# One layer of a hybrid encoder on one core: two products of the gates in another order, the scale of the scores moved into the keys, deeper loads of the last weights, a held split, and another order of the first instructions

## The chip, the core and the metric

The kernel runs on one core of a Trainium2 chip. The core has a matrix engine (TensorE, PE in the profile), a vector engine (DVE), an engine for activations and copies (ACT), a general engine (POOL, GpSimd) and an engine that issues most of the transfers (SP). The metric is device time in microseconds. The kernel before takes 869.28 us, the median of three runs (869.12 to 870.82).

## The reference: what is computed

The input is 512 rows of 1024 float32 values, one layer deep. Cut to what the change touches:

```python
n = rms_norm(h, mix_norm_g)
proj = n @ w_in                                    # S5 input, gMLP halves, two gates
gate_a, gate_b = sigmoid(proj[.., GA:GB]), sigmoid(proj[.., GB:])
merged = gate_a * (ya @ w_proj_a) + gate_b * (yb @ w_proj_b)
h = h + merged @ w_out
# memory cross-attention, 4 heads of 256, 256 memory tokens
s = einsum('blhd,bmhd->bhlm', q, k) * 256 ** -0.5
p = softmax(s)
h = h + einsum('bhlm,bmhd->blhd', p, v) @ w_xo
h = h + (silu(hn @ w_gate) * (hn @ w_up)) @ w_down # d_ff = 2816
return rms_norm(h, final_norm_g)
```

All of it is in float32.

## The kernel before, in words

**Matrix products.** Each float32 operand is split into two parts that TensorE multiplies in one pass: `hi` is a rounded copy (ACT, a CAST at L85) and `lo` the rest (DVE, a subtraction at L86). A product is three passes, hi*hi, hi*lo and lo*hi (`mm3`, L396). Weights come by DMA as blocks of 512 KB into `wraw` tiles, of which there are three (tag `raw`), and are split into `whi` and `wlo`.

**Strassen products.** The larger products are computed as seven products of half the size (Winograd's form), numbered 1 to 7. `product` (L1241) runs one of them; the banks in which sums build up are named `gx`, `gv`, `gq` for the gates, `qx`, `qv`, `qq` for the queries, `px`, `pv`, `pq` for the feed-forward part and `dx`, `dv`, `dq` for the down projection.

**What sets the order.** `plan` is a list of weight blocks in the order of their use. Each entry has loads, with how many entries ahead of its use each is issued (`LOADS` is 3), and a function that makes the split tiles, two entries ahead (`SPLITS`). `next_w` takes the next entry and starts what is due. The framework then orders the instructions of each engine with a simulated timeline; `in_order` keeps some in the order of the code, and `tc.issue_after(x)` holds some behind an instruction x. SP issues its DMAs strictly in that order: one that waits for a buffer holds up those behind it.

**The places in question.**
- Start (L590 to L640): ten matmuls on ones (`idle`), then two products of ones with the row of g (`pg`, which spreads g over the partitions), the first 128 rows scaled by DVE with `r` and `pg`, and in two halves: `whi` of the first weight block, a copy of `pg` into `g_mix`, the transposes of the rows (`ptr`, L563) with their split into `xn`, and `wlo`.
- Gates (L1323 on): `gate_step(q, i)` runs product q for gate i, in the order of the table `ORDER`. Step 7 copies `gx` on ACT and subtracts it from `gq` on DVE (`u`, L1254). Steps 1, 2, 4, 6 and 7 write `gx` or `gv`, steps 5 and 3 write `gq`.
- Attention (`k_evac`, `scores`): key tiles are split from the bank into `kt_hi` and `kt_lo`; for each head and each half of the rows, the scores `psc` are reduced to a maximum `mx`, `nm` is -scale times it, ACT forms exp(scale*psc + nm) with the sum `sm`, DVE the reciprocal `rs` and the scaled `prob`, and TensorE transposes `prob` (`ppt`, L1545).
- Down projection (`plan_down`): 42 entries, seven products of six blocks each; products 1, 2 and 3 read w_down itself, 5, 6, 7 and 4 read sums of its blocks that DMAs have built up in memory before (`dsum`). The pool `stp` holds the buffers of the feed-forward units before it (tags `b21`, `t`, `b22`, two each).
- End (`onto_h`, `make_tokens`): `onto_h(dx, 2, 0, ...)` adds the two banks of `dx` to h; `row_by_row(4, 0)` behind it asks for the tokens of product 4, which are split from `a_low` into `s`.

## Time and profile before

| | before |
|---|---|
| median of three runs | 869.28 us (869.12 to 870.82) |
| profiled execution, whole | 870.48 us |
| its span, first to last instruction | 868.7 us |
| busy: PE, DVE, ACT, POOL | 855.1, 648.3, 474.8, 106.0 us |
| TensorE matmuls | 5894 |
| mean granted TensorE clock | 0.996 |
| moved by DMA | 155.40 MB, mean 179 GB/s |

The busy time of an engine is the time in which at least one of its instructions ran. A wait is put down to the instruction that released it. In a row of the timeline the first two numbers are the start and the time taken, then come engine, line, operation, output and inputs, and in brackets the idle time ahead of it and what ended it. In the table by stretch, a row has the stretch, its length, the busy time and count of each engine, the granted clock, the share of the DMA engines that was busy, and GB/s.

### The profile page before, as it was taken

How to read it: one execution, taken by the hardware profiler on the slowest of the kernel's cores; microseconds unless marked ns; L12 is line 12 of the kernel's file. 1: busy time of each engine (PE TensorE's matmuls, PEld its weight loads, DVE VectorE, ACT ScalarE, POOL GpSimd, SP SyncE). 2: the span in 40 equal slices, each digit the busy share in tenths (PEclk: the TensorE clock that was granted, in tenths of full speed). 3: DMA queues.
4: the chain of work that ended last, by engine and by line, in shares of the span. 5: the costliest groups of instructions: out<-in, count | busy, mean ns of one | idle time of the engine just before them, and what ended most of it. 6: DMA issues, size and time to landing. Idle time of an engine off the chain costs nothing.

```text
span 868.7 us, 14845 instructions
## 1 busy us (share of the span) xinstructions
PE 855.1 (98%) x5894; PEld 760.1 (88%) x5894; DVE 648.3 (75%) x897; ACT 474.8 (55%) x704; POOL 106.0 (12%) x157
## 2 busy tenths in 40 slices
PE   8999999999999999999999999999999999999996
PEld 6788888888789988899899888999999999987875
DVE  5699589968748668679658646767877778898875
ACT  5544875276437534467457444655545454655664
POOL 1001155100601000110010001001111111000000
PEclk9999999999999999999999999999999999999999
DMA  7549279745639586944687143557798786476572
GB/s 247 163 115 265 66 216 242 160 128 169 158 92 252 138 230 206 274 124 160 217 257 214 53 151 103 146 146 178 166 240 230 183 222 143 134 213 216 201 246 94
DMA packets 110119, 155.40 MB, mean 179 GB/s; under 512 B 8969, under 2 KB 77089, under 8 KB 109986
## 3 DMA queue, kind: packets, MB, share of 16 engines
q1 hardware_dynamic: 91746, 128.27, 44.9%
q0 software_dynamic: 18016, 25.66, 18.5%
q8 instruction: 46, 0.75, 0.3%
q10 hardware_dynamic: 288, 0.52, 0.2%
q14 instruction: 23, 0.19, 0.1%
HBM read 148.70 MB, written 37.20 MB: 214 GB/s over the span
## 4 chain that ended last, share of the span: by engine, by line
PE 91%; DMA 3%; ACT 2%; DVE 2%; issue 1%; SPq 0%; POOL 0%; POOLq 0%; ACTq 0%; DVEq 0%
PE pf L396 25%; PE pt L396 18%; PE px L1241 13%; PE dx L396 7%; PE pq L1241 6%; PE pv L1241 3%; PE gx L1241 3%; PE qx L1241 3%; PE dq L396 2%; PE gq L1241 1%; PE psc L396 1%; PE po L396 1%; PE qq L1241 1%; PE py L1034 1%; PE ptr L563 1%
## 5 line engine op out<-in xcount | busy, mean ns | idle before, releaser
L85 ACT CAST whi<-wraw 128x1024 fp32r<-128x1024 f32 (+1 forms) x133 | 136.9, 1029 | 143.1 <-PE pf L396 42.1
L86 DVE TENSOR_TENSOR wlo<-wraw,whi 128x1024 fp32r<-128x1024 f32 (+1 forms) x133 | 158.5, 1192 | 71.9 <-ACT whi L85 70.9
L396 PE MATMUL pf<-xn,whi 128*128 128x512 f32 x320 | 99.8, 392 | 0.0
L1241 PE MATMUL px<-fn,whi 128*128 128x256 f32 x480 | 83.2, 276 | 0.0
L1241 PEld LDWEIGHTS px<-fn,whi 128*128 128x128 f32 x480 | 72.5, 188 | 0.2
L396 PEld LDWEIGHTS pf<-xn,whi 128*128 128x128 f32 x320 | 59.6, 188 | 12.5 <-issue 0.5
L85 ACT CAST whi<-b 128x1024 fp32r<-128x1024 f32 x40 | 42.2, 1054 | 51.4 <-PE px L1241 26.5
L86 DVE TENSOR_TENSOR wlo<-b,whi 128x1024 fp32r<-128x1024 f32 x40 | 48.9, 1222 | 28.5 <-ACT whi L85 28.5
L1241 PE MATMUL px<-fn,wlo 128*128 128x256 f32 x240 | 66.4, 277 | 0.0
L396 PE MATMUL pf<-xn,wlo 128*128 128x512 f32 x160 | 62.9, 393 | 0.0
L1241 PE MATMUL pq<-s,whi 128*128 128x256 f32 x320 | 55.0, 276 | 0.0
L396 PE MATMUL dx<-whi,s 128*128 128x512 f32 x170 | 53.3, 391 | 0.4 <-DVE h L1876 0.4
L86 DVE TENSOR_TENSOR wlo<-t,whi 128x1024 fp32r<-128x1024 f32 x30 | 36.7, 1224 | 19.4 <-ACT whi L85 19.4
L85 ACT CAST whi<-t 128x1024 fp32r<-128x1024 f32 x30 | 31.6, 1054 | 35.3 <-PE pv L1241 12.6
L1241 PEld LDWEIGHTS pq<-s,whi 128*128 128x128 f32 x320 | 48.2, 188 | 0.0
L1241 PEld LDWEIGHTS px<-fn,wlo 128*128 128x128 f32 x240 | 45.1, 188 | 0.0
L1241 PE MATMUL pq<-s,wlo 128*128 128x256 f32 x160 | 44.2, 276 | 0.0
L396 PE MATMUL pt<-whi,xn 128*128 128x512 f32 x128 | 42.8, 407 | 0.3 <-ACT xn L85 0.2
L396 PEld LDWEIGHTS dx<-whi,s 128*128 128x128 f32 x170 | 31.8, 188 | 7.6 <-issue 0.8
L312 POOL DMA_DIRECT2D dsum<-in_w_down_dram x12 | 13.3, 1108 | 189.8 <-DMA dsum<-in_w_down_dram 189.8
L396 PEld LDWEIGHTS pf<-xn,wlo 128*128 128x128 f32 x160 | 30.1, 188 | 6.3 <-issue 0.2
L396 PE MATMUL dx<-wlo,s 128*128 128x512 f32 x85 | 32.9, 389 | 0.0
(480 smaller groups left out, 2329.5 us busy)
## 6 DMA issues: line engine op xcount, KB each, us to landing
wraw<-in_w_in_dram SPq DMA_DIRECT2D x35, 512.0 KB, 5.8
dsum<-in_w_down_dram SPq DMA_DIRECT2D x20, 512.0 KB, 5.9
wraw<-dsum SPq DMA_DIRECT2D x20, 512.0 KB, 3.7
b<-in_w_gate_dram SPq DMA_DIRECT2D x15, 512.0 KB, 4.3
b<-in_w_up_dram SPq DMA_DIRECT2D x15, 512.0 KB, 5.2
wraw<-in_w_down_dram SPq DMA_DIRECT2D x15, 512.0 KB, 4.8
dsum<-in_w_down_dram POOLq DMA_DIRECT2D x10, 512.0 KB, 7.5
dsum<-dsum POOLq DMA_DIRECT2D x10, 512.0 KB, 6.4
```

The lines of the kernel that those rows point to most:

```text
L85: hi = nc.scalar.copy(dst_hi, src)
L86: lo = nc.vector.tensor_tensor(dst_lo, src, dst_hi.bitcast(F32), ALU.subtract)
L312: plan[j + step][1].append((0, lambda d=dst, x=more: nc.gpsimd.dma_start(d, x, accum_op=ALU.add)))
L396: last_mm[0] = nc.tensor.matmul(ps, a[x], b[y], start=start and i == 0, stop=stop and i == 2, skip_group_check=free)
L563: tr = nc.tensor.transpose(ps[:, j, :], src[:, k * P:(k + 1) * P], ident)
L1034: in_order(nc.tensor.matmul(ps[64 * j:64 * j + 64, :], a, b, start=g % 4 == k == 0, stop=k == 2, tile_position=(0, 64 * j), skip_group_che ...
L1241: nc.tensor.matmul(ps[:, j, :], a[x], b[y], start=start and j == k == i == 0, stop=k == 3 and i == 2, skip_group_check=True)
```

## The change

Six edits:

1. `ORDER`: the steps (3, 0) and (4, 0) change places.
2. The key tiles are scaled by -1/16 as they are split, and the scores then need a minimum and no multiplication.
3. `plan_down`: from the third entry on a load takes one of nine buffers in turn (three `raw`, two each of `b21`, `t`, `b22`) and is issued six entries ahead.
4. `held_back`: the token splits that `make_tokens` writes for product 4 after `onto_h(dx, 2, 0, ...)` are held behind the first addition of the latter.
5. The first weight block is loaded by two DMAs of 256 KB (`parts=2`).
6. Three idle matmuls ahead of the products of g and six behind, rather than ten ahead; the first half's `whi` and `wlo` are issued first, then both copies into `g_mix`, then the first half's transposes, the second half's weights and transposes.

```diff
@@ -130,12 +130,13 @@
         pad = pool.tile([P, 48], F32, name="pad", bufs=1)
         nc.gpsimd.memset(pad, 0.0)
 
-    def plan_block(w, kb, k, c0, n, more=None, place=None):
+    def plan_block(w, kb, k, c0, n, more=None, place=None, parts=1):
         got = {}
 
         def load():
             got["raw"] = wp.tile([P, k, n], F32, tag="raw", name="wraw", bufs=3)
-            nc.sync.dma_start(got["raw"], block(w, kb, k, c0, n))
+            for i in range(0, k, k // parts):
+                nc.sync.dma_start(got["raw"][:, i:i + k // parts], block(w, kb + i, k // parts, c0, n))
 
         def make():
             if more is not None:
@@ -150,7 +151,7 @@
 
     def plan_tok(w, c0, nk, kpt=2):
         for kb in range(0, nk, kpt):
-            plan_block(w, kb, kpt, c0, 512)
+            plan_block(w, kb, kpt, c0, 512, parts=1 if plan else 2)
 
 
 
@@ -222,7 +223,7 @@
             plan.append(((w_q, 512 * n, q), [(LOADS, load)], lambda got=got: halves(got.pop("raw"))))
 
     GATES = [(w_in, OFF_GB), (w_in, OFF_GB + 512)]
-    ORDER = ((1, 0), (1, 1), (2, 0), (2, 1), (5, 0), (6, 0), (5, 1), (7, 0), (6, 1), (3, 0), (7, 1), (4, 0), (4, 1), (3, 1))
+    ORDER = ((1, 0), (1, 1), (2, 0), (2, 1), (5, 0), (6, 0), (5, 1), (7, 0), (6, 1), (4, 0), (7, 1), (3, 0), (4, 1), (3, 1))
     gate_place = [None]
 
     def plan_gates():
@@ -312,20 +313,23 @@
             plan[j + step][1].append((0, lambda d=dst, x=more: nc.gpsimd.dma_start(d, x, accum_op=ALU.add)))
 
     def plan_down(w, make_tokens, entries):
+        turns = ("raw", "b21", "raw", "t", "b22", "raw", "b21", "t", "b22")
         for q in DOWN:
             for c in range(CHUNKS):
                 got = {}
 
-                def load(q=q, c=c, got=got):
+                def load(q=q, c=c, got=got, n=len(entries)):
                     src = down_block(*DSRC[q], c) if q in DSRC else down_sum(q, c)
-                    got["raw"] = wp.tile([P, 2, 512], F32, tag="raw", name="wraw", bufs=3)[:, :src.shape[1]]
+                    tag = turns[n % len(turns)] if n > 1 else "raw"
+                    got["raw"] = (wp if tag == "raw" else stp[0]).tile(
+                        [P, 2, 512], F32, tag=tag, name="wraw", bufs=3 if tag == "raw" else 2)[:, :src.shape[1]]
                     nc.sync.dma_start(got["raw"], src)
 
                 def make(q=q, c=c, got=got):
                     make_tokens(q, c)
                     return halves(got.pop("raw"))
 
-                entries.append(((w, q, c), [(LOADS, load)], make))
+                entries.append(((w, q, c), [(LOADS if len(entries) < 2 else 6, load)], make))
 
     plan_tok(w_in, OFF_V, KD)
     for c0 in range(0, SW, 256):
@@ -597,7 +601,7 @@
         for i in range(n):
             in_order(nc.tensor.matmul(idle, ones, ones, start=True, stop=True))
 
-    idles(10)
+    idles(3)
     warm = np_.tile([P, 1], F32, tag="ms", name="warm", bufs=2)
     nc.scalar.activation(warm, mhalf, AF.Square)
 
@@ -619,18 +623,25 @@
         pg = [aux("pg") for i in range(2)]
         for i in range(2):
             in_order(nc.tensor.matmul(pg[i], ones[0:1, :], g_row[:, HALF[i]], start=True, stop=True))
+        idles(6)
         r = rms_factor(row_sums(xt[:, 0, :]))
         raw = plan[0][3].pop("raw")
         hi = wp.tile([P, 2, 512], F32R, tag="hi", name="whi", bufs=3)
         lo = wp.tile([P, 2, 512], F32R, tag="lo", name="wlo", bufs=3)
         pinned[0] = True
+
+        def weights(q):
+            in_order(nc.scalar.copy(hi[:, q, :], raw[:, q, :]))
+            in_order(nc.vector.tensor_tensor(lo[:, q, :], raw[:, q, :], hi[:, q, :].bitcast(F32), ALU.subtract))
+
         for i in range(2):
             in_order(nc.vector.scalar_tensor_tensor(xt[:, 0, HALF[i]], xt[:, 0, HALF[i]], r, pg[i], ALU.mult, ALU.mult))
-        for q in range(2):
-            in_order(nc.scalar.copy(hi[:, q, :], raw[:, q, :]))
-            in_order(nc.scalar.copy(g_mix[:, HALF[q]], pg[q]))
-            to_feat(xt[:, 0, :], xn_hi, xn_lo, slice(0, P), part=(q,))
-            in_order(nc.vector.tensor_tensor(lo[:, q, :], raw[:, q, :], hi[:, q, :].bitcast(F32), ALU.subtract))
+        weights(0)
+        for i in range(2):
+            in_order(nc.scalar.copy(g_mix[:, HALF[i]], pg[i]))
+        to_feat(xt[:, 0, :], xn_hi, xn_lo, slice(0, P), part=(0,))
+        weights(1)
+        to_feat(xt[:, 0, :], xn_hi, xn_lo, slice(0, P), part=(1,))
         tiles.append((hi, lo))
 
     first_rows()
@@ -1460,8 +1471,11 @@
     kt_lo = ap_.tile([P, KD, M], F32R, name="kt_lo")
     vts = []
 
+    scale = XD ** -0.5
+
     def k_evac(m, j, ps):
-        split(kt_hi[:, m, :], kt_lo[:, m, :], ps)
+        nc.scalar.activation(kt_hi[:, m, :], ps, AF.Copy, scale=-scale)
+        nc.vector.scalar_tensor_tensor(kt_lo[:, m, :], ps, -scale, kt_hi[:, m, :].bitcast(F32), ALU.mult, ALU.subtract)
 
     def v_evac(half):
         def f(t, ps):
@@ -1512,7 +1526,6 @@
 
     def scores(hd, behind=None):
         q_hi, q_lo = qs.pop(hd)
-        scale = XD ** -0.5
         prob = ap_.tile([P, NT, M], F32, tag="prob", name="prob", bufs=1) if hd % 2 == 0 else \
             np_.tile([P, NT, M], F32, tag="gain", name="prob", bufs=2)
         for i in range(2):
@@ -1524,12 +1537,11 @@
                     with nullcontext() if behind is None else tc.issue_after(behind):
                         mm3(ps[:, tt, :], (q_hi[:, k, tsl], q_lo[:, k, tsl]),
                             (kt_hi[:, 2 * hd + k, :], kt_lo[:, 2 * hd + k, :]), k == 0, k == 1)
-            mx, nm, sm, rs = (ap_.tile([P, 2], F32, tag=k, name=k, bufs=4) for k in ("mx", "nm", "sm", "rs"))
-            nc.vector.tensor_reduce(mx, ps, AX.X, ALU.max)
-            nc.vector.tensor_scalar(nm, mx, -scale, None, ALU.mult)
+            nm, sm, rs = (ap_.tile([P, 2], F32, tag=k, name=k, bufs=4) for k in ("nm", "sm", "rs"))
+            nc.vector.tensor_reduce(nm, ps, AX.X, ALU.min)
             for tt in range(2):
                 nc.scalar.activation(prob[:, 2 * i + tt, :], ps[:, tt, :], AF.Exp, bias=nm[:, tt:tt + 1],
-                                     scale=scale, accum_out=sm[:, tt:tt + 1])
+                                     scale=-1.0, accum_out=sm[:, tt:tt + 1])
             nc.vector.reciprocal(rs, sm)
             for tt in range(2):
                 nc.vector.tensor_scalar(prob[:, 2 * i + tt, :], prob[:, 2 * i + tt, :], rs[:, tt:tt + 1], None, ALU.mult)
@@ -1738,7 +1750,7 @@
 
 
 
-    made, last_job = {}, []
+    made, last_job, held_back = {}, [], [None]
 
     def token_pieces(f, ts, c):
         if c < 2:
@@ -1753,7 +1765,8 @@
         hi, lo = made[q, c] = sums_place((1, 2, 4)[len(made) % 3], 4, 256)
         f, ts = {1: (0, T0), 5: (0, T1), 6: (0, T1), 2: (1, T0), 7: (0, T0), 3: (1, T0), 4: (1, T1)}[q]
         for src, ks in token_pieces(f, ts, c):
-            split(hi[:, ks], lo[:, ks], src)
+            with nullcontext() if held_back[0] is None else tc.issue_after(held_back[0]):
+                split(hi[:, ks], lo[:, ks], src)
         a, b_, c_, d_ = (token_pieces(f_, ts_, c) for ts_ in (T0, T1) for f_ in (0, 1))
         for (q11, _), (q12, _), (s21, _), (q22, _) in zip(a, b_, c_, d_):
             if q == 5:
@@ -1873,7 +1886,9 @@
     def onto_h(ps, t0, half, op):
         for t in range(2):
             hs = h[:, t0 + t, HALF[half]]
-            nc.vector.tensor_tensor(hs, hs, ps[t], op)
+            added = nc.vector.tensor_tensor(hs, hs, ps[t], op)
+            first = added.ins if t == 0 else first
+        return first
 
     def row_by_row(q, c0):
 
@@ -1901,12 +1916,13 @@
         finish(t)
     down_product(dx, 7, False, range(CHUNKS - 2))
     row_by_row(7, CHUNKS - 2)
-    onto_h(dx, 2, 0, ALU.subtract)
+    held_back[0] = onto_h(dx, 2, 0, ALU.subtract)
     for t in range(2, 4):
         first_half(t, 0)
 
     held = []
     row_by_row(4, 0)
+    held_back[0] = None
     for c in range(2, CHUNKS):
         ops_ = next_w(w_down, 4, c)
         if c < CHUNKS - 2:
```

How this moves instructions. TensorE at the start, its first instructions (`idle` and `pg` as above, `pt` the first product), before and after:

```order
L598 MATMUL idle<-ones 128x128 x10
L621 MATMUL pg<-g_row,ones 128x512 x2
L563 MATMUL ptr<-ident,xt 128x128 x8
L396 MATMUL pt_259<-whi,xn 128x512
L396 MATMUL pt_259<-wlo,xn 128x512
```

The same engine at the same place after the change:

```order
L602 MATMUL idle<-ones 128x128 x3
L625 MATMUL pg<-g_row,ones 128x512 x2
L602 MATMUL idle<-ones 128x128 x6
L567 MATMUL ptr<-ident,xt 128x128 x8
L400 MATMUL pt_259<-whi,xn 128x512
L400 MATMUL pt_259<-wlo,xn 128x512
```

Six of ten idle products move behind `pg`, between it and the transposes, and one goes.

DVE in the attention, from the reduction of the second head's second half (`psc_4850` before, `psc_4844` after) to the scaling of its `prob`:

```order
L1528 TENSOR_REDUCE mx_4863<-psc_4850 128x2
L86 TENSOR_TENSOR wlo_5024<-wraw_4794,whi_5023 128x1024
L86 TENSOR_TENSOR qq_4874<-u3_4710,qq_4874 128x2x256
L1529 TENSOR_SCALAR nm_4864<-mx_4863 128x2
L86 TENSOR_TENSOR qq_4874<-u2_4626,qq_4874 128x2x256
L86 TENSOR_TENSOR ot_lo_4880<-po_4881,ot_hi_4879 128x512
L86 TENSOR_TENSOR ot_lo_4880<-po_4890,ot_hi_4879 128x512
L1528 TENSOR_REDUCE mx_4913<-psc_4900 128x2
L1533 RECIPROCAL rs_4866<-sm_4865 128x2
L1528 TENSOR_REDUCE mx_4937<-psc_4924 128x2
L1529 TENSOR_SCALAR nm_4914<-mx_4913 128x2
L1535 TENSOR_SCALAR prob_4825<-prob_4825,rs_4866 128x256 x2
```

The same engine at the same place after the change:

```order
L1541 TENSOR_REDUCE nm_4857<-psc_4844 128x2
L86 TENSOR_TENSOR wlo_5008<-wraw_4790,whi_5007 128x1024
L86 TENSOR_TENSOR qq_4866<-u3_4706,qq_4866 128x2x256
L86 TENSOR_TENSOR qq_4866<-u2_4626,qq_4866 128x2x256
L1545 RECIPROCAL rs_4859<-sm_4858 128x2
L86 TENSOR_TENSOR ot_lo_4872<-po_4873,ot_hi_4871 128x512
L1547 TENSOR_SCALAR prob_4821<-prob_4821,rs_4859 128x256 x2
L86 TENSOR_TENSOR ot_lo_4872<-po_4882,ot_hi_4871 128x512
L1541 TENSOR_REDUCE nm_4905<-psc_4892 128x2
L1541 TENSOR_REDUCE nm_4927<-psc_4914 128x2
```

The `nm` instructions are gone, and the scaling of this `prob` stands ahead of the reductions of the next head's two score tiles rather than behind them.

SP from the last sums to the first loads of the down projection (`dsum5` are the sums of product 5; the entries of the down projection are numbered by their tiles, in the order of use 7763, 7831, 7837, 7872, 7890, 7921, 7945 after, and 7927 the third before):

```order
L322 DMA wraw_7847<-in_w_down_dram 128x2x512
L322 DMA wraw_7927<-in_w_down_dram 128x2x512
L322 DMA wraw_7948<-in_w_down_dram 128x2x512
L311 DMA dsum4_83<-in_w_down_dram 128x2x512
L322 DMA wraw_7984<-in_w_down_dram 128x2x512
L322 DMA wraw_8023<-in_w_down_dram 128x512
L322 DMA wraw_8046<-dsum5_84 128x1024
L322 DMA wraw_8064<-dsum5_84 128x1024
L322 DMA wraw_8087<-dsum5_84 128x1024
```

The same engine at the same place after the change:

```order
L326 DMA wraw_7945<-dsum5_84 128x1024
L312 DMA dsum4_83<-in_w_down_dram 128x2x512
L326 DMA wraw_7831<-in_w_down_dram 128x2x512
L326 DMA wraw_7872<-in_w_down_dram 128x2x512
L326 DMA wraw_7890<-in_w_down_dram 128x2x512
L326 DMA wraw_8062<-dsum5_84 128x1024
L326 DMA wraw_7837<-in_w_down_dram 128x2x512
L326 DMA wraw_7921<-in_w_down_dram 128x512
L326 DMA wraw_8040<-dsum5_84 128x1024
```

The first load of product 5 (7945) now stands ahead of the second block of product 1, and a later one (8062) ahead of the third (7837).

DVE at the end, around the two additions of `dx` to `h` (`s2` are the tokens of product 4):

```order
L86 TENSOR_TENSOR wlo_8690<-wraw_8666,whi_8689 128x1024
L86 TENSOR_TENSOR s2_8729<-a_low_5466,s2_8729 128x1024
L1876 TENSOR_TENSOR h_3416<-h_3416,dx0_7880 128x512
L1876 TENSOR_TENSOR h_3416<-h_3416,dx1_7881 128x512
L86 TENSOR_TENSOR wlo_8696<-wraw_8684,whi_8695 128x1024
L1836 TENSOR_TENSOR rest_7519<-h_3416,g_o_8016 128x512 x2
```

The same engine at the same place after the change:

```order
L86 TENSOR_TENSOR wlo_8678<-wraw_8593,whi_8677 128x1024
L1889 TENSOR_TENSOR h_3416<-h_3416,dx0_7866 128x512
L86 TENSOR_TENSOR s2_8717<-a_low_5450,s2_8717 128x1024
L1889 TENSOR_TENSOR h_3416<-h_3416,dx1_7867 128x512
L86 TENSOR_TENSOR wlo_8684<-wraw_8619,whi_8683 128x1024
L1849 TENSOR_TENSOR rest_7503<-h_3416,g_o_8006 128x512
```

The token split moves from ahead of the first addition to between the two.

## The prediction

> **What bounds the kernel now.** I read the page first, then the waits of TensorE, then the timeline around each of them. The page's rows for TensorE and for the chain that ended last:
> ```profile
> span 868.7 us, 14845 instructions
> PE 855.1 (98%) x5894; PEld 760.1 (88%) x5894; DVE 648.3 (75%) x897; ACT 474.8 (55%) x704; POOL 106.0 (12%) x157
> PE 91%; DMA 3%; ACT 2%; DVE 2%; issue 1%; SPq 0%; POOL 0%; POOLq 0%; ACTq 0%; DVEq 0%
> ```
> TensorE is the bound nearly everywhere, so an edit that neither removes matmuls nor ends an idle stretch of TensorE is worth nothing. Its waits (line, releaser: total us, times, longest):
> ```profile
> PE pf L396 <- ACT yb_hi L85: 1.4, 1, 1.4
> PE ppt L1545 <- DVE prob L1535: 1.1, 1, 1.1
> PE dv L396 <- DVE wlo L86: 0.5, 1, 0.5
> PE ptr L563 <- ACT g_mix L631: 0.4, 1, 0.4
> PE dx L396 <- DVE h L1876: 0.4, 1, 0.4
> PE gq L1241 <- DVE u L1254: 0.4, 1, 0.4
> PE dv L396 <- ACT whi L85: 0.3, 1, 0.3
> PE pt L396 <- DVE wlo L633: 0.3, 1, 0.3
> ```
> The first row, 1.4 us, is not touched. The others are what the change can win: 1.1 + 0.5 + 0.4 + 0.4 + 0.4 + 0.3 + 0.3 = 3.4 us, and the start beyond its listed waits. The profiled run took 870.48 us, 1.78 around the span, 1.20 above the median of 869.28. I make the sum as a difference and take it off the median; 0.2% is 1.74 us, about what this kernel's times can tell from no change.
>
> **Gates.** The order of two products changes.
> ```profile
> 286.79 0.58 ACT L1250 COPY u<-gx 128x512 f32<-128x512 f32 x1
> 288.06 0.68 DVE L1254 TENSOR_TENSOR u<-gq,u 128x512 f32<-128x512 f32 x1
> 288.80 0.39 PE L1241 MATMUL gq<-gsd,whi 128*128 128x256 f32 x1 [0.41 <-DVE u L1254]
> ```
> Now TensorE goes from product (6,1) to (3,0), which writes the bank `gq` that DVE reads until 288.74. After, (4,0) comes first: it writes `gx`, which ACT has copied by 287.37, 0.8 us before TensorE gets there. The weights of (4,0) come from a GpSimd accumulation issued long before, and ACT's cast takes the slot the other product's cast had. (3,0) runs two products later, when `u` is long done. Gain 0.41, with the restart of the pipelined matmuls perhaps 0.58; I take 0.5. At the other end, weights that land late: 0.
>
> **Attention.** The scale of the scores moves into the key tiles, with its sign, so `mx` and the multiplication to `nm` become one minimum: eight small DVE instructions go. That is little work; what counts is where they stood.
> ```profile
> 476.43 0.16 DVE L1529 TENSOR_SCALAR nm<-mx 128x2 f32<-128x2 f32 x1
> 476.64 0.48 ACT L1531 ACTIVATE prob<-psc,nm 128x256 f32<-128x256 f32 x1
> 479.34 0.69 DVE L1528 TENSOR_REDUCE mx<-psc 128x2 f32<-128x512 f32 x1 [0.28 <-PE psc L396]
> 480.01 0.61 DVE L1535 TENSOR_SCALAR prob<-prob,rs 128x256 f32<-128x256 f32 x2
> L86 DVE TENSOR_TENSOR kt_lo<-pf,kt_hi x8: 412/416/418, 389.4 to 412.2; 128x256 fp32r<-128x256 f32 x8
> ```
> `nm` ran behind two splits at 476.43, its exponential at 476.64, and the scaling of `prob` behind the next head's reduction (until 480.03); TensorE's transposes would have started about 479.3. After, the exponential follows the reduction directly and moves ahead of two `ot_hi` casts on ACT, some 1.5 us earlier, and DVE scales `prob` ahead of both later reductions: ready about 478.4, so the 1.1 us go. What is late next: the next head's transposes. TensorE reaches them 1.1 us sooner, while the `p_hi` cast now stands ahead of that head's exponentials on ACT; adding up the durations of ACT and DVE in their new order I find `prob` about 0.3 us late. Net 0.9, ends 0.4 and 1.28. The eight `kt_lo` subtractions become operations with a scalar, which are about a tenth dearer (0.77 for each of the two of 6.68 below, of 128x512, against 0.68 for `u` above): 8 x 0.04 = 0.3 us on a DVE that TensorE does not wait for there. Were that cover gone, they cost 0.3.
>
> **Loads of the last weights.** From three buffers and three entries ahead to nine buffers and six ahead.
> ```profile
> 784.78 0.37 SPq L322 DMA_DIRECT2D wraw<-in_w_down_dram  x1
> 792.29 1.05 ACT L85 CAST whi<-wraw 128x1024 fp32r<-128x1024 f32 x1 [3.02 <-DMA wraw<-in_w_down_dram]
> 727.00:760.00 33.00, 33.00 (x266) 31.78 (x265) 26.13 (x26) 19.67 (x23) 0.81 (x1) 1.00 0.42 118
> 760.00:800.00 40.00, 39.19 (x173) 31.54 (x171) 35.22 (x42) 22.26 (x28) 1.62 (x2) 1.00 0.71 210
> ```
> The load issued at 784.78, as soon as one of three buffers was free, landed 7.5 us later, and ACT and TensorE stood (0.3 and 0.5 us). With six more buffers this load goes out some 15 us earlier, into the stretch before, in which the DMA engines were busy 0.42 of the time (second number from the right) rather than 0.71. Both waits go, 0.81; with the restarts up to 1.5; I take 1.1. The other end, that a later load is late instead: 0.
>
> **The held split at the end.** DVE now adds `dx` to `h` ahead of a token split.
> ```profile
> 844.36 1.22 DVE L86 TENSOR_TENSOR s<-a_low,s 128x1024 fp32r<-128x1024 f32 x1
> 845.76 1.29 DVE L1876 TENSOR_TENSOR h<-h,dx 128x512 f32<-128x512 f32 x2 [0.18 <-PE dx L396]
> 846.59 0.47 PE L396 MATMUL dx<-whi,s 128*128 128x512 f32 x1 [0.42 <-DVE h L1876]
> ```
> The split ended at 845.58 and the add waited 0.18 us more, for TensorE: its last matmul on `dx0` comes two matmuls before the stall, and their order does not change. So the add starts no earlier without the split ahead of it, and the 0.4 us stay. The split, 1.22 us, moves between the two adds, and the second add then ends about 848.2, just when TensorE wants `dx1` (seven matmuls of 0.23 after 846.59). I take 0, ends +0.4 and -0.3.
>
> **Start.** The first weight block comes as two DMAs, three idle products stand ahead of g's two products and six behind instead of ten ahead, both g copies run before the rows' casts, and two small DVE operations and the first `wlo` move forward.
> ```profile
> 1.06 4.46 PE L598 MATMUL idle<-ones 128*128 128x128 f32 x20 [1.06 <-DVE dcol L828]
> 5.45 1.98 PE L621 MATMUL pg<-g_row,ones 1*128 1x512 f32 x4
> 7.48 0.66 PE L563 MATMUL ptr<-ident,xt 128*128 128x128 f32 x4
> 6.68 1.53 DVE L628 SCALAR_TENSOR_TENSOR xt<-xt,r,pg 128x512 f32<-128x512 f32 x2 [1.02 <-PE pg L621]
> 7.41 0.62 ACT L630 CAST whi<-wraw 128x512 fp32r<-128x512 f32 x1 [2.13 <-DMA wraw<-in_w_in_dram]
> 9.89 0.61 ACT L85 CAST xn<-ptr 128x512 fp32r<-128x512 f32 x1
> 12.96 1.05 ACT L85 CAST whi<-wraw 128x1024 fp32r<-128x1024 f32 x1 [0.29 <-DMA wraw<-in_w_in_dram]
> 13.88 1.41 DVE L643 SCALAR_TENSOR_TENSOR xt<-xt,r,g_mix 128x512 f32<-128x512 f32 x2 [0.67 <-POOL r L534]
> 15.21 1.22 DVE L86 TENSOR_TENSOR wlo<-wraw,whi 128x1024 fp32r<-128x1024 f32 x1
> xt<-in_x_dram ACTq DMA_DIRECT2D x1, 256.0 KB, 2.5
> 8.00:10.00 2.00, 1.56 (x7) 1.02 (x5) 1.17 (x3) 2.00 (x6) 0.00 (x0) 0.65 1.01 396
> 10.00:12.00 2.00, 1.72 (x5) 0.96 (x4) 1.80 (x4) 2.00 (x6) 0.00 (x0) 0.50 1.03 391
> ```
> The ten idle products take 0.45 us each, so three end at 2.4. When g's row lands is not shown: before 5.45; by the nearest row, a load of the same moment that took 2.5 us, about 3.2. g's products took 1.98 us for four pieces of 512 columns where twenty idle pieces of 128 took 4.46: the clock had doubled by then. Starting at 3.2, half cold, they end about 6; six idle products add 1.3 us warm or 2.7 cold, so the transposes start at 7.3 or 8.7, against 7.48. In the warm case ACT has done its first cast (half the block lands sooner) and both copies before the transposes; the second half's transposes no longer wait (0.4 us), and the cast of 9.89 moves to about 9.0. The chain behind it (squares on ACT, `r` on POOL, the scaling of 13.88, `wlo` of 15.21) moves with it, 0.9 us. Its floor is the third block's cast, which waited for a saturated DMA until 12.96; `wlo` after it can end at 15.3, so 0.9 passes. In the cold case the cast of 9.89 comes 0.5 us later. I take the warm case, +0.9, since the hole of 0.8 us leaves TensorE busy four fifths of the first 4.4 us; the ends are -0.5 and +0.9. The additional DMA shifts SP's later issues by some 0.4 us (0.37 at 784.78); their transfers stand in a full DMA (shares 1.01 to 1.03), which hides that.
>
> The granted clock (third number from the right) fell to 0.65 and 0.50 between 8 and 12 us, behind the waits at 7.4 to 8.6. [...]
>
> **Sum.** 0.5 + 0.9 + 1.1 + 0 + 0.9 = 3.4 us off 869.28: 865.9 (the profiled run would read 867.1).
>
> **Rivals.**
> - The start goes cold: 865.9 + 0.9 + 0.5 = 867.3. [...]
> - The waits move on: the next head takes back 0.7 of the 1.1, a later load in the down stage another 0.8, the start gives 0.4. Then 0.5 + 0.4 + 0.3 + 0 + 0.4 = 1.6: 867.7, or less gain still, to 869.0. For it speaks that DVE is busy 35.22 of 40 us in the down stage; against it that a wait there was on a DMA.
> - Slower: SP's queue. SP issues in order, and one load for a buffer of the last weight unit now stands ahead of the next plain load.
> ```profile
> 744.16 2.06 SPq L322 DMA_DIRECT2D wraw<-in_w_down_dram  x2
> 754.66 1.05 ACT L85 CAST whi<-wraw 128x1024 fp32r<-128x1024 f32 x1 [0.86 <-PE dx L396]
> ```
> That plain load is issued at 744.16 and used at 754.66: 10.5 us, 7.5 of them for a slow landing, so 3 us to spare. If the buffer ahead came free later than 747, each microsecond more would stall TensorE one. By the profile it is free at 743.0. To end 1.74 slower against gains of 3.4 it would need 752: 871 or more.
>
> **How the numbers follow.** As forecast 0.50 (864.4 to 867.0); cold start 0.20; waits that move on 0.17; SP's queue 0.08; 0.05 for what I don't see. Faster by over 0.2% (below 867.54): 0.50 + 0.14 of the cold start + 0.03 = 0.67. Within: 0.17 + 0.06 = 0.23. Slower: 0.08 + 0.02 = 0.10. The range goes from 864.2 (all terms at their good ends: 0.58 + 1.28 + 1.5 + 0.4 + 0.9 = 4.7, and a little) to 869.0.
>
> **What would show it.** Among TensorE's waits those on `u`, on `g_mix` and both at `dv` are gone; the one at `ppt` is 0.5 or less; the one on `h` is still 0.4. In the down stage no cast waits for a load. The first cast on ACT starts before 6.5, the first transposes at 7.3, the third block's `wlo` ends near 15.5. Wrong would make it: transposes at 8.5 or later, a clock of 0.5 before 8 us, a new wait on `prob` of 1 us, or casts that wait for `wraw` after 743.

## The result and the profile after

The changed kernel takes 868.27 us in the median (867.28 to 870.19), the kernel before, on the same chip and in turn with it, 870.34 (868.35 to 874.2). The ratio is 0.9973 with a 95% interval of 0.9964 to 0.9982: 0.27% faster, 2.3 us of the 3.4 that were forecast. 868.27 lies in the range on record. That range was laid from a median of 869.28; the kernel before stood 1.06 us higher this time, so the gain is read from the ratio. 0.27% off 869.28 would be 866.9, in the range too.

The page of the changed kernel, its span, its busiest engines and the chain that ended last:

```profile
span 866.5 us, 14830 instructions
PE 855.0 (99%) x5892; PEld 760.5 (88%) x5892; DVE 646.8 (75%) x889; ACT 476.0 (55%) x704; POOL 108.4 (13%) x157
PE 95%; ACT 2%; DMA 1%; issue 1%; DVE 0%; SPq 0%; POOL 0%; POOLq 0%; ACTq 0%
```

TensorE has 91% of the chain before and 95% now; DMA falls from 3% to 1%, DVE from 2% to nothing. Its waits (line, releaser: total us, times, longest):

```profile
PE pf L400 <- ACT yb_hi L85: 1.5, 1, 1.5
PE idle L602 <- DVE level L844: 1.1, 1, 1.1
PE pt L400 <- DVE wlo L86: 0.8, 1, 0.8
PE pt L400 <- ACT xn L85: 0.5, 2, 0.2
PE dx L400 <- DVE h L1889: 0.4, 1, 0.4
```

Those on `prob`, `u`, `g_mix` and both at `dv` are gone; the one on `h` has stayed. New is 0.8 us on a `wlo`, and that lies in the start, at 13.1 us. Where the time went is seen best when every matmul is compared with the same matmul of the kernel before. The start of it after the change, less its start in the profile shown of before (the median of 25 neighbours, worked out from the two traces):

```
at (us)     shift (us)   what lies between this row and the one above
30           +0.60       the start
200          +0.67
230          +0.82       the wait on yb_hi at 218, which the change does not touch
300          +0.14       the gates: -0.68
476          +0.47       the attention ahead of the transposes: +0.33
490          -0.83       the transposes of prob: -1.30
780          -0.64       no single wait: +0.19
800          -2.22       the last weights: -1.58
858          -2.14       the end: +0.08
```

So three edits gain 0.68 + 0.97 + 1.58 and the start loses 0.6 against this profile, 0.9 + 0.6 less than forecast. At the start, TensorE after the change:

```profile
1.06 1.65 PE L602 MATMUL idle<-ones 128*128 128x128 f32 x6 [1.06 <-DVE level L844]
2.64 3.78 PE L625 MATMUL pg<-g_row,ones 1*128 1x512 f32 x4
6.35 2.93 PE L602 MATMUL idle<-ones 128*128 128x128 f32 x12
9.07 1.38 PE L567 MATMUL ptr<-ident,xt 128*128 128x128 f32 x8
```

g's row has landed by 2.64, earlier than the 3.2 of the forecast. But its products take 3.78 us where the kernel before had 1.98, the six idle products 2.93, and the transposes begin at 9.07 where it had 7.48. They could have begun earlier: both halves of their input `xt` were ready by 7.8 (the first row below), and it was TensorE's own six idle products that still stood ahead of them. The rows behind are those that answer the casts and the third block's `wlo` shown of before:

```profile
6.38 1.41 DVE L638 SCALAR_TENSOR_TENSOR xt<-xt,r,pg 128x512 f32<-128x512 f32 x2 [0.55 <-POOL r L538]
5.99 0.62 ACT L634 CAST whi<-wraw 128x512 fp32r<-128x512 f32 x1 [0.66 <-DMA wraw<-in_w_in_dram]
10.05 0.59 ACT L85 CAST xn<-ptr 128x512 fp32r<-128x512 f32 x1 [1.65 <-PE ptr L567]
16.21 1.22 DVE L86 TENSOR_TENSOR wlo<-wraw,whi 128x1024 fp32r<-128x1024 f32 x1
```

ACT's first cast runs at 5.99 (7.41 before) and both halves of the first block are there in time. From 7.16 to 8.40 ACT copies g, then it waits 1.65 us for TensorE. What was to become earlier by 0.9 us became later: the cast of 9.89 is at 10.05, and the `wlo` that began at 15.21 begins at 16.21.

In the attention and the gates, the rows that answer those of before:

```profile
475.52 0.47 ACT L1543 ACTIVATE prob<-psc,nm 128x256 f32<-128x256 f32 x1
477.80 0.61 DVE L1547 TENSOR_SCALAR prob<-prob,rs 128x256 f32<-128x256 f32 x2
287.61 0.58 ACT L1261 COPY u<-gx 128x512 f32<-128x512 f32 x1
288.88 0.68 DVE L1265 TENSOR_TENSOR u<-gq,u 128x512 f32<-128x512 f32 x1
```

`prob` is done at 478.41, where 478.4 was forecast, and no transposes wait, the next head's included. The addition to `u` runs as late as ever (288.88), but TensorE now computes another bank meanwhile. The down stage, in two windows (TensorE busy comes behind the length, the share of the DMA engines second from the right), and the rows of the end:

```profile
727.00:760.00 33.00, 33.00 (x263) 31.73 (x262) 26.05 (x26) 19.78 (x24) 0.81 (x1) 1.00 0.73 217
760.00:800.00 40.00, 40.00 (x178) 33.15 (x177) 37.52 (x45) 24.21 (x30) 1.63 (x2) 1.00 0.74 223
```

```profile
843.54 0.69 DVE L1889 TENSOR_TENSOR h<-h,dx 128x512 f32<-128x512 f32 x1 [1.32 <-PE dx L400]
844.15 1.22 DVE L86 TENSOR_TENSOR s<-a_low,s 128x1024 fp32r<-128x1024 f32 x1
844.38 0.47 PE L400 MATMUL dx<-whi,s 128*128 128x512 f32 x1 [0.42 <-DVE h L1889]
```

The loads have moved into the stretch before (share of the DMA engines 0.73 at 727 to 760, where it was 0.42), TensorE has no idle time left at 760 to 800 (40.00 of 40, before 39.19), and between 743 and 850 no cast of ACT waits for a load any more; before, 15 did. At the end DVE now waits 1.32 us for `dx` with the add, and TensorE stands 0.42 us as before.

### The profile page after: what moved, and what is told of

Same layout as the page of the kernel before. It is cut to its first block, busy times and chain, and to the rows that moved or that the text cites. A ratio compares the mean times of both kernels' runs of the same rounds, so it can differ in the third digit from the quotient of the medians.

```text
span 866.5 us, 14830 instructions
## 1 busy us (share of the span) xinstructions
PE 855.0 (99%) x5892; PEld 760.5 (88%) x5892; DVE 646.8 (75%) x889; ACT 476.0 (55%) x704; POOL 108.4 (13%) x157
## 4 chain that ended last, share of the span: by engine, by line
PE 95%; ACT 2%; DMA 1%; issue 1%; DVE 0%; SPq 0%; POOL 0%; POOLq 0%; ACTq 0%
PE pf L400 25%; PE pt L400 18%; PE px L1252 13%; PE dx L400 7%; PE pq L1252 6%; PE dq L400 3%; PE pv L1252 3%; PE gx L1252 3%; PE qx L1252 3%; PE dv L400 2%; PE ptr L567 1%; PE psc L400 1%; PE po L400 1%; PE qq L1252 1%; PE gq L1252 1%; PE py L1045 1%
```

## The experiments

A ratio is to the kernel before on the same chip; shifts are worked out as above, against the profile shown of before unless it is said otherwise. The 95% interval of every ratio below overlaps with that of the changed kernel (0.9964 to 0.9982), so by these medians alone no run can be told from the changed kernel with certainty. What one edit does is read from the traces, and each trace is one execution.

**The start put back, all else changed.** The two halves are one DMA again, ten idle products stand ahead of g's, and the casts and copies are in the old order:

```
-            plan_block(w, kb, kpt, c0, 512, parts=1 if plan else 2)
+            plan_block(w, kb, kpt, c0, 512, parts=1)
...
-    idles(3)
+    idles(10)
...
-        idles(6)
...
-        weights(0)
-        for i in range(2):
-            in_order(nc.scalar.copy(g_mix[:, HALF[i]], pg[i]))
-        to_feat(xt[:, 0, :], xn_hi, xn_lo, slice(0, P), part=(0,))
-        weights(1)
-        to_feat(xt[:, 0, :], xn_hi, xn_lo, slice(0, P), part=(1,))
+        for q in range(2):
+            in_order(nc.scalar.copy(hi[:, q, :], raw[:, q, :]))
+            in_order(nc.scalar.copy(g_mix[:, HALF[q]], pg[q]))
+            to_feat(xt[:, 0, :], xn_hi, xn_lo, slice(0, P), part=(q,))
+            in_order(nc.vector.tensor_tensor(lo[:, q, :], raw[:, q, :], hi[:, q, :].bitcast(F32), ALU.subtract))
```

> The changed kernel with the start of the kernel before: one load of the first weight block, ten idle products ahead of g's, the old order of the casts, copies and weights. Theory (the six idle products behind g's run at half rate and hold the transposes; in the traces the start is 0.6 us later after the change, everything else 2.7 us earlier): 2.7 us less than the kernel before, 0.6 us less than the changed kernel, the transposes at 7.5 us. Rival (the start's edits are worth nothing or a gain in most executions, and the profiled one was unlucky): no less than the changed kernel, some 2.1 us less than before.

Measured 867.79 us, ratio 0.9978 (0.9967 to 0.9989). In its trace the transposes begin at 7.43, and at 30 us the shift is -0.21, 0.8 better than with the changed start. By the medians the two starts can't be told apart (0.9973 and 0.9978, each by about 0.0010): the run came out 1.9 us below the kernel before, which is nearer to the rival's 2.1 than to the theory's 2.7. The traces say only that in these profiled executions the new start is the later one.

**Ten idle products ahead of g's, none behind; the rest of the new start kept.**

```
-    idles(3)
+    idles(10)
...
-        idles(6)
```

> The changed kernel with all ten idle products ahead of g's and none behind; the two loads, the early copies and the order of the weights stay. Theory (the idle products' place is what costs): the clock has doubled when g's products run, the transposes start at 7.1 to 7.5 rather than 9.07 and no longer wait for the copies, the third block's lower part ends near 15.5 rather than 17.4; 1.5 us less than the changed kernel (1.0 to 1.9), 3.7 less than before. Rival (it is the two loads or the order of the casts): the transposes as late as in the changed kernel, and no less time.

TensorE at the start of this kernel:

```profile
1.05 4.23 PE L602 MATMUL idle<-ones 128*128 128x128 f32 x20 [1.05 <-DVE level L843]
5.21 1.98 PE L625 MATMUL pg<-g_row,ones 1*128 1x512 f32 x4
7.59 1.83 PE L567 MATMUL ptr<-ident,xt 128*128 128x128 f32 x8 [0.40 <-DVE xt L637]
```

Measured 866.26 us, ratio 0.9965 (0.9952 to 0.9979). g's products take 1.98 us again, the transposes begin at 7.59, now held by `xt` for 0.40 us, and the shift at 30 us is -0.74, which is 1.34 us better than the change. In this trace the other edits of the start (two DMAs, copies first, the earlier `wlo`) are thus worth most of the 0.9 us that were forecast, and the place of the idle products costs more than that. The third block's `wlo` ends at 16.08, later than the 15.5 expected. The medians can't show the gain: against the kernel before it is 3.0 us (1.8 to 4.2), where 3.7 were expected and the change has 2.3.

**Eight idle products ahead, none behind.**

```
-    idles(3)
+    idles(8)
...
-        idles(6)
```

> As the run with ten, with eight idle products. Theory: if the clock has doubled by the time g's products run, they end 0.9 us earlier, but DVE then waits for r, near 6.3, so the transposes start at 7.1 and it is the same as with ten within 0.3 us. Rival (the shorter run of idle products leaves the clock at half rate until 8.6): g's products end near 7, the transposes at 7.8 or later, 0.5 us more than with ten.

Measured 867.22 us, ratio 0.9968 (0.9956 to 0.9979); shift -0.92 at 30 us. g's products run at 4.38, in 1.98 us, and the transposes at 7.42 wait 1.06 us for `xt`. Two idle products fewer do not slow g's products (full rate, 0.109 us a piece rather than 0.213, came at 3.9, where the rival had 8.6) and gain no more than 0.2 us, since `xt` is the limit then. Eight and ten can't be told apart here.

**The additions of `dx` apart at the end.** Row 1's last products of `dx` are kept behind all of row 0's, so that DVE can add `dx0` to `h` while row 1 is still computed:

```
-    def row_by_row(q, c0):
+    def row_by_row(q, c0, apart=False):
...
-                rows_product(dx, q, c, ops_, (t,), slice(0, 512), False, c == CHUNKS - 1)
+                with tc.issue_after(row1) if apart and t == 1 else nullcontext():
+                    rows_product(dx, q, c, ops_, (t,), slice(0, 512), False, c == CHUNKS - 1)
+            row1 = last_mm[0].ins
...
-    row_by_row(7, CHUNKS - 2)
+    row_by_row(7, CHUNKS - 2, True)
```

> The changed kernel with TensorE's matmuls on the second bank of dx, in the last two blocks of product 7, held behind all of those on the first bank. Theory (the 0.4 us wait at the end belongs to TensorE's order, since the addition waits for the first bank and only two matmuls cover it): the addition to h starts 1.2 us earlier relative to the stalled matmul and the wait of dx for h is gone; a wait of up to 0.2 us for the second addition may take its place; 0.2 to 0.5 us less than the changed kernel. Rival (the wait is the split's or DVE's doing): the wait of 0.4 us stays.

DVE at the end of this kernel:

```profile
841.21 0.68 DVE L1889 TENSOR_TENSOR h<-h,dx 128x512 f32<-128x512 f32 x1
841.81 1.22 DVE L86 TENSOR_TENSOR s<-a_low,s 128x1024 fp32r<-128x1024 f32 x1
```

Measured 867.09 us, ratio 0.9966 (0.9954 to 0.9979). The first add now waits for nothing and TensorE's wait on `h` is gone; the shift goes from -3.15 at 842 to -3.82 at 845. These 0.67 us are more than the 0.42 of the wait, since the matmuls also start again slowly behind it: in the changed kernel the first one there is followed after 0.31 us, the ones ahead of the wait every 0.227. It shows that the wait of 0.42 us hung on when TensorE gave `dx0` free, as the prediction has it, not on DVE's order.

**The held split put back.**

```
-    held_back[0] = onto_h(dx, 2, 0, ALU.subtract)
+    onto_h(dx, 2, 0, ALU.subtract)
```

> The changed kernel without the hold on the token split. Theory (the split was never what the addition waited for): the wait of 0.42 at dx is as before, and the time that of the changed kernel within what it can tell, 0 to 0.1 us less. Rival (the hold helps by something the wait doesn't show): more than 0.3 us more than the changed kernel between 840 and 860.

Measured 867.18 us, ratio 0.997 (0.9956 to 0.9983). The end of this kernel:

```profile
842.41 1.22 DVE L86 TENSOR_TENSOR s<-a_low,s 128x1024 fp32r<-128x1024 f32 x1
843.81 1.28 DVE L1889 TENSOR_TENSOR h<-h,dx 128x512 f32<-128x512 f32 x2 [0.18 <-PE dx L400]
844.64 0.47 PE L400 MATMUL dx<-whi,s 128*128 128x512 f32 x1 [0.42 <-DVE h L1889]
```

With the split ahead of the add DVE waits 0.18 us for `dx`, without it 1.32, and TensorE stands 0.42 us either way. The shift is the same at 838 and 858. The edit is worth nothing.

**The old order of the gates' products.**

```
-    ORDER = ((1, 0), (1, 1), (2, 0), (2, 1), (5, 0), (6, 0), (5, 1), (7, 0), (6, 1), (4, 0), (7, 1), (3, 0), (4, 1), (3, 1))
+    ORDER = ((1, 0), (1, 1), (2, 0), (2, 1), (5, 0), (6, 0), (5, 1), (7, 0), (6, 1), (3, 0), (7, 1), (4, 0), (4, 1), (3, 1))
```

> The changed kernel with the old order of the gate steps. Theory (the wait on u is the order's): the wait of 0.41 at gq is back, the stretch from 280 to 300 us is 0.6 to 0.7 us longer than in the changed kernel, everything else as there. Rival (the wait had gone by an earlier or later arrival): no wait.

Measured 868.34 us, ratio 0.9979 (0.9967 to 0.9992). The wait is back, in TensorE's row of this kernel:

```profile
289.23 0.39 PE L1252 MATMUL gq<-gsd,whi 128*128 128x256 f32 x1 [0.41 <-DVE u L1265]
```

Between 284 and 300 us this kernel falls 0.68 us behind the changed one: 0.41 of wait and 0.27 of restart (the first matmul behind the wait is followed after 0.22 us, the later ones every 0.113).

**The old softmax in the attention.** The scale goes back from the key tiles to the scores, `mx` and `nm` are two instructions again:

```
-        nc.scalar.activation(kt_hi[:, m, :], ps, AF.Copy, scale=-scale)
-        nc.vector.scalar_tensor_tensor(kt_lo[:, m, :], ps, -scale, kt_hi[:, m, :].bitcast(F32), ALU.mult, ALU.subtract)
+        split(kt_hi[:, m, :], kt_lo[:, m, :], ps)
...
-            nc.vector.tensor_reduce(nm, ps, AX.X, ALU.min)
+            nc.vector.tensor_reduce(mx, ps, AX.X, ALU.max)
+            nc.vector.tensor_scalar(nm, mx, -scale, None, ALU.mult)
```

> The changed kernel with maximum, multiplication and scale as before in the attention. Theory (the nm instructions and what they put off are the cause): the wait of 1.1 us at ppt is back, the stretch from 476 to 490 us 1.3 us longer; and, if the slower spacing of TensorE's matmuls there (0.118 rather than 0.1135 us from 465 to 476, 0.33 us in all) comes with the edit, that stretch is 0.3 us shorter, 1.0 us net. Rival for the spacing (it has nothing to do with the edit): the spacing stays at 0.118 there, 1.3 us net.

Measured 868.68 us, ratio 0.9983 (0.9973 to 0.9992). `prob` is scaled at 479.86 and the transposes wait:

```profile
480.26 0.70 PE L1557 MATMUL ppt<-ident,prob 128*128 128x128 f32 x4 [1.11 <-DVE prob L1547]
```

Against the changed kernel this one is 0.3 us ahead at 465, 0.62 at 476, then 0.66 behind at 490 (the rows between are the transposes): it gets back the 0.3 us that the edit loses ahead of them, and loses 1.3 us there. Net, the edit gains about 0.97. All nine traces with the new softmax lose the 0.3 us between 465 and 476; this one, the three of the kernel before and that with the early loads alone do not.

**The loads of the last weights as before, all else changed.** Three buffers and three entries ahead:

```
-        turns = ("raw", "b21", "raw", "t", "b22", "raw", "b21", "t", "b22")
...
-                    tag = turns[n % len(turns)] if n > 1 else "raw"
-                    got["raw"] = (wp if tag == "raw" else stp[0]).tile(
-                        [P, 2, 512], F32, tag=tag, name="wraw", bufs=3 if tag == "raw" else 2)[:, :src.shape[1]]
+                    got["raw"] = wp.tile([P, 2, 512], F32, tag="raw", name="wraw", bufs=3)[:, :src.shape[1]]
...
-                entries.append(((w, q, c), [(LOADS if len(entries) < 2 else 6, load)], make))
+                entries.append(((w, q, c), [(LOADS, load)], make))
```

> The changed kernel with three buffers for the last weights and loads three entries ahead, as before. Theory (the load in the middle of the down stage is late for want of a buffer): a cast waits 3 us for its load near 790, TensorE 0.3 and 0.5 us, the stretch from 780 to 798 us is 1.6 us longer than in the changed kernel. Rival (that load was late by the traffic of one execution): no wait, the same time.

Measured 868.23 us, ratio 0.9978 (0.9967 to 0.999). The wait that was to come back did not: TensorE has none at `dv`, and the shift across 780 to 800 is -1.48, nearly that of the changed kernel. ACT's casts around the place:

```profile
784.75 1.05 ACT L85 CAST whi<-wraw 128x1024 fp32r<-128x1024 f32 x1 [0.92 <-DMA wraw<-in_w_down_dram]
788.70 1.05 ACT L85 CAST whi<-wraw 128x1024 fp32r<-128x1024 f32 x1 [2.08 <-DMA wraw<-in_w_down_dram]
```

The casts still wait for loads, as in the kernel before, but here the load issued at 783.25 landed 5.45 us later, where that of 784.78 had taken 7.5. So the profile shown of before may have been an unlucky one.

**The kernel before again, twice.** Not a line changed.

> The kernel before, once more, for its trace: was the late load of the down stage (issued 784.78, landed 7.5 us later, TensorE 0.3 and 0.5 us idle) that kernel's or that execution's? With the loads undone in the changed kernel the same load landed after 5.4 us and nothing waited. Theory (the three buffers leave some 6 us, and the landing varies between 5 and 8): a landing time other than 7.5 and a wait that differs, perhaps none. Rival (the rest of the kernel before, which stands otherwise against its transfers, makes it late each time): 7 us or more again, TensorE idle 0.8 us at dv.

> As the run before it, a third execution. Theory: the landing of that load is again another; over the three executions the wait at dv is not the same. Rival: the wait of 0.8 us in all three.

They took 870.28 and 868.86 us. TensorE's longer waits outside the start, in the first and in the second of them:

```profile
PE ppt L1545 <- DVE prob L1535: 1.1, 1, 1.1
PE pf L396 <- ACT yb_hi L85: 0.9, 1, 0.9
PE dv L396 <- DVE wlo L86: 0.5, 1, 0.5
PE dx L396 <- DVE h L1876: 0.4, 1, 0.4
PE gq L1241 <- DVE u L1254: 0.4, 1, 0.4
```

```profile
PE ppt L1545 <- DVE prob L1535: 1.1, 1, 1.1
PE pf L396 <- ACT yb_hi L85: 0.6, 1, 0.6
PE dx L396 <- DVE h L1876: 0.4, 1, 0.4
PE gq L1241 <- DVE u L1254: 0.4, 1, 0.4
```

The waits on `prob`, `h` and `u` are the same in all three executions. The stalls at `dv` are not: two of 0.5 and 0.3 us, then one of 0.5, then none. Nor is it the same load. In the second execution ACT's casts show that the load of the forecast, issued at 785.96 there, landed in time after 4.0 us (the second row), and that the stall came from the load three places earlier in the queue, issued at 777.51 and landed after 6.1 (the first row):

```profile
783.62 1.05 ACT L85 CAST whi<-wraw 128x1024 fp32r<-128x1024 f32 x1 [1.02 <-DMA wraw<-in_w_down_dram]
789.98 1.06 ACT L85 CAST whi<-wraw 128x1024 fp32r<-128x1024 f32 x1
```

In the third the load of the forecast was issued at 783.34, and its cast at 788.66 did not wait for it. So with three buffers it varies which load is late, and whether one is. Counted from the stretch 780 to 800, where the kernel with all loads early is 1.57 us ahead of the profile shown, the three lose 1.6, 1.1 and 0 us there, 0.9 in the mean; that is more than the waits themselves, since the matmuls around a wait follow each other more slowly too (in the profile shown the first one behind each of the two waits is followed after 0.34 us, where 0.227 is the spacing further off). The start differs too: at 30 us the two are 0.68 and 0.37 later than the profile shown, which was the fastest start of the three.

**The early loads alone, in the kernel before.** The lines of the weights' loads above, turned round and put into the kernel before:

```
-                entries.append(((w, q, c), [(LOADS, load)], make))
+                entries.append(((w, q, c), [(LOADS if len(entries) < 2 else 6, load)], make))
```

> The kernel before with the nine buffers and the loads six ahead, and no other edit. Theory (what is won is the wait at dv where it occurs): no wait at dv or dx for a load; between 0 and 1.6 us less than the kernel before, by how often the load is late there. Rival (the deeper loads cost elsewhere, by traffic or SP's queue): more time than before, or casts that wait for wraw.

Measured 869.31 us, ratio 0.9987 (0.9975 to 0.9999): 0.13%, 1.1 us, between 0.1 and 2.2. No matmul waits for a load in the down stage. The mean of 0.9 us lies inside this. The start of this trace, which the edit does not touch, was the slowest of all (shift +2.06 at 30 us): behind the same ten idle products g's products took as long as in the changed kernel:

```profile
5.62 3.78 PE L624 MATMUL pg<-g_row,ones 1*128 1x512 f32 x4
```

**Both improvements together:** ten idle products ahead and none behind, and the rows apart.

```
-    idles(3)
+    idles(10)
...
-        idles(6)
...
-    row_by_row(7, CHUNKS - 2)
+    row_by_row(7, CHUNKS - 2, True)
```

> Ten idle products ahead of g's and none behind, and dx's two banks apart: the two edits that each took a wait away. Theory (they lie 830 us apart and add): 4.3 us less than the kernel before (3.6 to 5.2), some 2 us less than the changed kernel. Rival (what is won at the start is given back at a wait further on, such as the one of 0.6 to 1.5 us at 218): 3 us less than before, no more than either alone.

Measured 866.14 us, ratio 0.9958 (0.9943 to 0.9974), the lowest of all kernels here by the median, 0.42% below the kernel before. That is 3.7 us (2.3 to 5.0) where 4.3 were expected and the rival had 3; the interval holds both, and the medians don't show that the two gains add. From the list of TensorE's waits:

```profile
PE pf L400 <- ACT yb_hi L85: 1.6, 1, 1.6
PE pt L400 <- ACT xn L85: 0.5, 2, 0.3
PE ptr L567 <- DVE xt L653: 0.4, 1, 0.4
```

Both gains are in its trace (shift -0.61 at 30 us, and 0.67 more between 842 and 845, across the wait on `h`, which is gone). Of the rest only the first row, behind GpSimd's clearing of `bd`, is worth more than half a microsecond outside the start.

## Why the prediction was right, and where it was wrong

**Gates: right.** 0.68 us by the trace and by the run without the edit, and as much in the other traces with the new order; 0.5 was taken. The restart of the pipelined matmuls is 0.27 us on 0.41 of wait, more than the 0.17 that the good end of 0.58 allowed.

**Attention: right in sum, wrong in what is late next.** `prob` was ready at 478.41, as forecast, and the whole wait went, with its restart 1.30 us. The 0.3 us that came off again were expected at the next head's transposes; these do not wait. They are lost ahead of the transposes, from 465 to 476 us, where TensorE's matmuls follow each other every 0.118 us instead of every 0.1135 with no wait between them. The run without the edit does not have this, so it comes with the edit. What slows them was not found: the granted clock reads 1.00 in both. The eight `kt_lo` operations, taken as a tenth dearer, are not: 416 ns each before and after.

**Loads of the last weights: the mechanism right, its size an accident of one execution.** All waits on loads went, and 1.58 us against the profile shown is the good end of the range (1.5), not the 1.1 taken. But the stall that was costed is one that the kernel before has in some executions and not in others, and not at the same load each time; over three of them it costs 0.9, and the run with this edit alone gained 1.1 us with a wide interval. The fourth trace with three buffers, of the run with the loads put back, loses 0.1. A median against a median should get something near that 0.9, not 1.6.

**Held split: right.** Forecast 0 because the add waits for TensorE and not for DVE's split; taking the edit back moved nothing, and letting TensorE free `dx0` earlier took the wait away.

**Start: wrong, and this is the step that failed.** The prediction took the warm case "since the hole of 0.8 us leaves TensorE busy four fifths of the first 4.4 us". That so much busy time brings full rate was the author's estimate, and no run shows it. In its place the runs showed half rate without any hole: g's row had landed by 2.64 and TensorE went from the three idle products straight to g's. It was busy without a break from 1.06 to 10.2, and its pieces still came every 0.213 us until 9.7 (0.109 after that). So the cold rival, with a chance of 0.20, is what happened, though not by way of the hole: transposes at 9.07 where it had 8.7, and a loss of 0.6 us against the profile shown where it had 0.5. The sign that was named for it, transposes at 8.5 or later, is there; the other, a clock of 0.5 before 8 us, is not, because the profile's clock column reads 1.00 over these microseconds while the durations show half rate.

How much of that loss is in the medians is less certain. At 30 us the changed start is 0.60 to 0.96 us behind the profile shown in six traces of it. The old start, in five traces (three of the kernel before, that with the early loads alone, that with the start put back), is at 0, +0.68, +0.37, +2.06 and -0.21; the +2.06 is an old start that went cold too. Against the three of the kernel before, the new start loses some 0.4 us in the mean (0.75 less 0.35), against all five 0.2. With ten or eight idle products in front the start was cold less often: g's products took 3.8 us in all six traces with three in front, and 3.78 in one of the eight traces with ten or eight; in the other seven they took 1.98 to 2.29.

**The sum.** With the mean of three executions for the loads and the loss of 0.4 for the start: 0.68 + 0.97 + 0.9 + 0 - 0.4 = 2.2 us, against 2.3 measured (1.6 to 3.1). The loads and the start are means over few traces that differ by more than a microsecond, so that the two agree so closely is in part luck. Of the forecast of 3.4 the start took 1.3, the loads 0.2, and the gates gave 0.2 back. The rival on SP's queue did not come: no cast and no matmul waits for a load between 743 and 850.

## What to carry to other kernels

A single profile of the kernel before is one draw: a wait on a DMA that the kernel catches by a microsecond should be looked for in a second and a third execution before it is entered into a sum, while TensorE's waits on DVE (here 1.1, 0.4 and 0.4 us) came back to the tenth of a microsecond in all three executions. Here the idle products were worth most in one unbroken block ahead of g's products: with eight or ten there these took 1.98 to 2.29 us in seven traces of eight, with three there and six behind 3.8 in six traces of six. Ten in a block were no guarantee either: in one trace g's products took 3.78 us behind them. The edit on an engine that itself waits (DVE for `dx0`) was worth nothing; the edit that makes the bank free earlier was the one that paid (0.67 us).

## What the runs showed of the hardware

**TensorE reached full rate at different times, once not before 17 us.** The windows of the changed kernel (TensorE busy and its count first, then weight loads, DVE, ACT, POOL, the granted clock, the DMA share, GB/s), and then those of the kernel before:

```profile
2.40:6.40 4.00, 4.00 (x7) 1.23 (x6) 0.45 (x5) 1.99 (x7) 0.56 (x1) 1.00 0.94 336
6.40:9.70 3.30, 3.30 (x16) 3.30 (x16) 1.99 (x3) 1.38 (x3) 0.00 (x0) 1.00 1.00 384
```

```profile
2.40:6.40 4.00, 4.00 (x18) 3.40 (x18) 0.31 (x2) 1.57 (x6) 0.55 (x1) 1.00 0.93 311
6.40:9.70 3.30, 2.81 (x12) 1.63 (x10) 2.16 (x4) 2.29 (x5) 0.00 (x0) 0.83 1.02 383
9.70:12.00 2.30, 2.02 (x5) 0.96 (x4) 2.10 (x5) 2.30 (x6) 0.00 (x0) 0.50 1.03 391
```

In the changed kernel 16 pieces of 128 columns take 3.30 us, 0.21 each, while the column says 1.00; the single records show 0.213 us from one piece to the next until 9.71 and 0.109 after that, in the midst of the transposes. In the kernel before that change came at 5.2, behind 4.1 us of idle products, and g's products took 1.98 us behind it; with eight idle products in front it came at 3.9, behind 2.8 us of them, with 1.98 us again. So in the changed kernel it was not for want of being busy: TensorE ran 1.6 us of idle products, from 2.64 to 6.35 g's products (`1*128` in their row), in 3.78 us, then idle products again, and full rate came at 9.71. Nor did it last in the kernel before, where the second transposes, from 8.6 on, came every 0.213 us again; its clock column reads 0.50 from 9.70 to 12.00, and in its two repeats from 10 to 14.

Behind the same ten idle products full rate came between 4.7 and 6.3 us in six traces, and at 17.0 in the trace of the early loads alone, though the row of its idle products has 4.63 us without a break. What sets the time is not shown by these traces. A run in which g's row is multiplied on all 128 rows, which would tell whether it matters that g's products have one, was not made.

**One wait moves by a microsecond from execution to execution.** TensorE's wait at 218 us, which no edit touches, was 1.4, 0.9 and 0.6 us in the three profiles of the kernel before, 1.5 after the change and 0.4 to 1.7 in the other kernels. In the changed kernel ACT's queue there:

```profile
218.65 0.60 ACT L873 COPY bd<-bbr 64x128 f32<-64x128 f32 x2 [4.13 <-POOL bd L870]
...
219.90 0.62 ACT L85 CAST yb_hi<-zu 128x512 fp32r<-128x512 f32 x1
```

The cast that TensorE wants stands on ACT behind copies that wait 4.13 us for GpSimd to clear `bd`. By its size this is the next thing to change, and it was not tried. Runs of one kernel differ by more than the whole change was forecast to bring (868.35 to 874.2 us for the kernel before). This wait, the late loads and the time at which TensorE reaches full rate are three things that move in the traces by one or two microseconds each; how much of the spread they make was not measured.
